# Gates and branch projections by tokens instead of by features in a four-branch mixer, finer attention steps, and another set of durations in the planner's clock

## The chip, the cores and the metric

The kernel runs on one core of a Trainium2 chip. The metric is the device time of one execution in microseconds (us). TensorE (PE) multiplies, with the weight load of each multiplication as a separate instruction (PEld) beside it; VectorE (DVE), ScalarE (ACT) and GpSimd (POOL) do the elementwise work; SyncE (SP) issues the transfers from HBM.

## The reference, cut to what matters

256 tokens with 1024 features go through two layers of one kind (a) and two of another (b). Both kinds have a mixer of four branches, whose outputs are projected to 1024 features, gated, summed and projected again:

```python
# kind a                                        # branches of 512 features
ys = jnp.stack([y_ssm, y_fox, y_moba, y_dsa], axis=2)
proj = jnp.einsum('bsnc,ncd->bsnd', ys, w_branch)
gates = jax.nn.sigmoid(h @ w_gate + b_gate).reshape(bsz, seq, N_BRANCH, D_MODEL)
merged = jnp.sum(gates * proj, axis=2)
return merged @ w_out
...
# kind b                                        # branches of 256 features
o_a = mla_branch(cq, ckv, kpe, positions, mla_norm_q, mla_norm_kv, mla_w_uq, mla_w_ukv)
o_b = spatial_gating_branch(sg_uv, sg_ln_g, sg_ln_b, sg_w, sg_b)
o_c = gla_branch(gq, gk, gv, g_lr, g_og, gla_w_gate, gla_b_gate, gla_norm)
o_d = deltanet_branch(dq, dk, dv, da, db, dz, dn_conv, dn_a_log, dn_dt_bias, dn_norm)
proj = jnp.einsum('bsnw,nwd->bsnd', branches, w_branch)
gate = jax.nn.sigmoid(gates).reshape(b, s, N_BRANCH, D_MODEL)
merged = jnp.sum(gate * proj, axis=2)
return merged @ w_out
```

Kind a then has a SwiGLU layer, kind b a cross attention and a squared-ReLU layer. Three of a's branches and b's `mla_branch` and cross attention are softmax attention over heads of 64.

## The kernel before

**Matrix products.** All of it is fp32. A large product splits each operand in a high and a low part of a reduced fp32 type and takes three passes on PE (high times high, high times low, low times high), so a contraction step of 128 is three matmuls into one PSUM bank. These are the matmuls with `rt` operands in the rows; the small ones of the branches work on `ft` operands in plain fp32. A tile of weights of 128x1024 comes by DMA into one of four `raw` slots, ACT writes its high part (`rt<-raw`), DVE its low part (`rt<-raw,rt`), at most five tiles ahead of PE. A result that becomes the next left operand is split in the same way, by an ACT copy and a DVE subtraction.

**The order of the work** is not written by hand. A planner writes the program twice: it keeps a rough clock (`Model`) that adds up a duration for each instruction (`Engine.cost`, L371, and the transfer's duration in `dma`, L430) and, between the matmuls of large products, takes steps from "lanes", generators that do the branches' small work and `yield` between steps. `spawn` adds such a generator, `drain` runs all of them (or until a flag is set) with no large product between, `flush` runs those of a key. Engines execute in the written order, each its own queue.

**The mixer** (`mix`, L1400) runs for both kinds. It goes through the branches in a fixed order, `ORDER1` = (2, 1, 3, 0) for kind a, `ORDER2` = (1, 0, 2, 3) for kind b, where 2 is GLA and 3 is DeltaNet, and through two halves of 512 output features of each. For a half, `gate` multiplies `h` by the gate weights over 8 contraction steps and `proj` the branch's output over 4 (a) or 2 (b). `proj` begins with `if n not in flags: self.drain(until=lambda: n in flags)`: where the branch isn't ready, its lane is run down first. The products stand with features on partitions: a bank holds two blocks of 128 features by 256 tokens, so a matmul has 256 columns, and a half is two banks (`g2`). The gate's tanh on ACT takes the bias of kind a as a per-partition operand, two instructions of 256 columns for each bank. `stt` on DVE computes (tanh + 1) times the projection out of PSUM. Sums over branches run on POOL, and for the last branch on DVE; `fin` splits the sum into high and low parts as a spawned step with the key `mT0` to `mT3`.

Behind the mixer, `layer_a` and `layer_b` call `self.drain()`, which runs down all lanes; then `out_a` (L1454, token halves of 128, 512 columns) or `out_b` (L2231) multiplies by `w_out`, and flushes the key of each part of the sum before it uses it.

**Attention** (`attention`, L855) takes two heads at a time in a lane step: the second product of pair i-2, the transposes and copies (`pt`) of pair i-1, and the scores, maximum, exponential, reciprocal and scaling of pair i, then one `yield`.

**Head norms** of GLA and DeltaNet (`head_norm`, L1618) go through a matmul, ACT square, DVE reduction, a power on POOL, and DVE scaling, with transposes on PE behind.

Of the kernel before, what the change touches and what calls it, by code (L numbers as in the profile page):

```python
# [9 lines left out]
F32R = mybir.dt.float32r  # L10
# [3 lines left out]
AF = mybir.ActivationFunctionType  # L14
# [3 lines left out]
D = 1024  # L18
# [48 lines left out]
def plan(layer):  # L67
# [9 lines left out]
    if kind == "a":  # L77
# [5 lines left out]
        for i, n in enumerate(ORDER1):  # L83
            for w, c in (("g", 0), ("p", 0), ("g", 1), ("p", 1)):
# [18 lines left out]
    else:  # L103
# [4 lines left out]
        for i, n in enumerate(ORDER2):  # L108
            for w, c in (("g", 0), ("p", 0), ("g", 1), ("p", 1)):
# [242 lines left out]
class Engine:  # L352
# [38 lines left out]
class Kern:  # L391
# [463 lines left out]
    def attention(self, heads, qk, sel, bias, v, dst, done):  # L855
# [16 lines left out]
        for i in range(n + 2):  # L872
# [15 lines left out]
            if 1 <= i <= n:  # L888
# [10 lines left out]
                st[("pt", i - 1)] = pts  # L899
            if i < n:  # L900
# [18 lines left out]
                for j in range(2):  # L919
# [66 lines left out]
    def params(self, layer):  # L986
# [8 lines left out]
        if kind == "a":  # L995
            load("pp", 72, dram["pp1"][l])
# [40 lines left out]
    def layer_a(self, l, hT, pr):  # L1037
# [347 lines left out]
        bg = F.alloc(32, "bg")  # L1385
        self.ts(bg.a, pp[:, 40:72], 0.5, OP.mult)
# [4 lines left out]
        merged = self.mix(L, l, ORDER1, hT, ys, flags, 4, bg.a, load_gains)  # L1391
        bg.free()
# [7 lines left out]
    def mix(self, L, l, order, hT, ys, flags, nkt, bias, load):  # L1400

        F = self.F
        mg, m = {}, []
        halves = [[(256 * g, 256 * g + 128), (256 * g + 128, 256 * g + 256)] for g in range(2)]

        def gate(n, c):
# [19 lines left out]

        def proj(i, n, c, gts):
            if n not in flags:
                self.drain(until=lambda: n in flags)
            for g in range(2):  # L1430
# [1250 lines left out]
```

## Time and profile before

| | |
|---|---|
| median of 3 runs | 2298.11 us (2293.02 to 2301.42) |
| profiled execution | 2296.01 us, span of its trace 2294.2 us |
| mean granted TensorE clock | 0.991 of full speed |
| PE busy | 2237.2 us, 98% |
| PEld busy | 2020.1 us, 88% |
| DVE busy | 1526.5 us, 67% |
| ACT busy | 1074.2 us, 47% |
| POOL busy | 271.2 us, 12% |
| DMA | 375.47 MB, mean 164 GB/s |

PE is busy nearly always, so the time is read as PE's queue: the durations of its instructions, and the places where it stands idle, with what it waited for. All instructions go through one helper, so every row carries L362; what they are is told by engine, operation, tile and shape.

### The profile page before, as it was taken

Reading aid. Unit: us, or ns where it says so; the run is one execution under the profiler, and the core shown is the slowest. Engines: PE = TensorE matmul, PEld = TensorE weight load, DVE = VectorE, ACT = ScalarE, POOL = GpSimd, SP = SyncE. Lnnn points to the kernel's source line nnn. Section 1 sums busy time; section 2 is a strip of 40 time slices with the busy share of each in tenths; the row PEclk is TensorE's granted clock in tenths of the full one; section 3 lists DMA queues with packets and bytes.
Section 4 is the critical chain, followed back from the end, with each engine's and each line's share of the span. In section 5 each row is a group of like instructions: output and inputs, shape, how many; then the busy total and the mean of one; then the engine's idle time right before and its main releaser. Section 6 shows DMA issues by size and latency. Waiting matters only on the chain.

```text
span 2294.2 us, 40097 instructions
## 1 busy us (share of the span) xinstructions
PE 2237.2 (98%) x16244; PEld 2020.1 (88%) x16244; DVE 1526.5 (67%) x2509; ACT 1074.2 (47%) x1695; POOL 271.2 (12%) x244
## 2 busy tenths in 40 slices
PE   7999999999999999999999999999999999999998
PEld 6888998999787899889988899988988889998897
DVE  7786657555888655755588867555557887755554
ACT  4554544444455444544454345444545433544543
POOL 3002120000301112000021321000002132000000
PEclk9999999999999999999999999999999999999999
DMA  6433555555534356565544246456653424644563
GB/s 224 140 122 118 184 183 194 198 182 168 174 118 147 110 166 202 174 228 187 171 132 155 86 131 218 144 177 221 195 165 113 156 94 136 214 155 157 193 204 108
DMA packets 106662, 375.47 MB, mean 164 GB/s; under 512 B 12474, under 2 KB 12908, under 8 KB 106476
## 3 DMA queue, kind: packets, MB, share of 16 engines
q1 hardware_dynamic: 106476, 372.91, 49.4%
q8 instruction: 127, 2.08, 0.4%
q14 instruction: 59, 0.48, 0.1%
HBM read 371.81 MB, written 1.05 MB: 163 GB/s over the span
## 4 chain that ended last, share of the span: by engine, by line
PE 63%; DVE 6%; issue 2%; ACT 1%; DMA 1%; POOL 1%; SPq 0%; POOLq 0%; DVEq 0%; ACTq 0%
PE bank L362 63%; DVE ft L362 4%; DVE rt L362 2%; POOL ft L362 1%; ACT rt L362 1%; ACT ft L362 0%; DMA raw<-in_wts_a 0%; DMA raw<-in_wts_b 0%; DMA ft<-in_positions 0%; POOL qt L362 0%; ACT junk L362 0%; SPq L430 0%; DVE junk L362 0%; POOLq L2676 0%; DVEq L362 0%
## 5 line engine op out<-in xcount | busy, mean ns | idle before, releaser
L362 PE MATMUL bank<-rt 128*128 128x256 f32 (+2 forms) x12720 | 1993.5, 316 | 28.0 <-DVE rt L362 27.7
L362 PEld LDWEIGHTS bank<-rt 128*128 128x128 f32 x12720 | 1781.1, 192 | 186.2 <-DVE rt L362 34.7
L362 DVE TENSOR_TENSOR rt<-raw,rt 128x1024 fp32r<-128x1024 f32 (+2 forms) x692 | 837.5, 1239 | 343.5 <-ACT rt L362 342.3
L362 ACT ACTIVATE rt<-raw 128x1024 fp32r<-128x1024 f32 (+2 forms) x692 | 698.7, 1034 | 410.4 <-PE bank L362 213.5
L362 POOL TENSOR_TENSOR ft<-ft 128x512 f32<-128x512 f32 (+7 forms) x186 | 213.1, 1153 | 1879.7 <-DVE ft L362 1673.5
L362 PE MATMUL bank<-ft 64*64 64x64 f32 (+11 forms) x3476 | 315.6, 266 | 18.8 <-DVE ft L362 12.0
L362 PEld LDWEIGHTS bank<-ft 64*64 64x64 f32 (+6 forms) x3476 | 243.7, 147 | 74.5 <-issue 16.0
L362 ACT ACTIVATE ft<-bank 128x512 f32<-128x512 f32 (+5 forms) x256 | 135.7, 536 | 317.6 <-PE bank L362 290.2
L362 ACT ACTIVATE ft<-ft 128x128 f32<-128x128 f32 (+7 forms) x206 | 87.5, 434 | 182.5 <-DVE ft L362 175.7
L362 DVE SCALAR_TENSOR_TENSOR ft<-ft 128x512 f32<-128x512 f32 (+5 forms) x211 | 93.6, 465 | 42.0 <-ACT junk L362 20.5
L362 DVE TENSOR_TENSOR ft<-ft 128x512 f32<-128x512 f32 (+5 forms) x122 | 68.3, 562 | 63.0 <-ACT ft L362 60.6
L362 DVE SCALAR_TENSOR_TENSOR ft<-bank,ft 128x254 f32<-128x254 f32 (+6 forms) x176 | 80.5, 482 | 24.5 <-PE bank L362 13.9
L362 ACT ACTIVATE rt<-bank 128x512 fp32r<-128x512 f32 (+1 forms) x98 | 53.6, 552 | 85.1 <-PE bank L362 84.1
L362 DVE TENSOR_TENSOR ft<-ft,bank 64x512 f32<-64x512 f32 (+3 forms) x92 | 59.3, 645 | 36.0 <-PE bank L362 29.6
L362 ACT ACTIVATE ft<-bank,ft 128x256 f32<-128x256 f32 x108 | 47.2, 481 | 72.0 <-PE bank L362 48.6
L362 DVE SCALAR_TENSOR_TENSOR ft<-ft,bank 128x512 f32<-128x512 f32 (+1 forms) x106 | 67.6, 642 | 14.6 <-PE bank L362 9.9
L362 DVE COPY ft<-bank 128x384 f32<-128x384 f32 (+6 forms) x96 | 49.4, 542 | 32.9 <-PE bank L362 30.4
L362 DVE TENSOR_SCALAR ft<-ft 128x256 f32<-128x256 f32 (+7 forms) x236 | 55.4, 277 | 21.3 <-ACT ft L362 9.8
L362 ACT ACTIVATE rt<-ft 128x512 fp32r<-128x512 f32 x62 | 39.0, 630 | 65.0 <-DVE ft L362 60.5
L362 DVE TENSOR_TENSOR ft<-bank,ft 128x512 f32<-128x512 f32 (+8 forms) x124 | 50.3, 442 | 16.1 <-PE bank L362 7.5
L362 POOL TENSOR_SCALAR qt<-qt,ft 64x256 fp32r<-64x256 f32 (+1 forms) x32 | 42.1, 1318 | 131.4 <-PE bank L362 130.5
L362 ACT ACTIVATE junk<-ft 128x512 bf16<-128x512 f32 (+1 forms) x46 | 27.2, 591 | 58.1 <-DVE ft L362 55.6
(37 smaller groups left out, 318.6 us busy)
## 6 DMA issues: line engine op xcount, KB each, us to landing
raw<-in_wts_a SPq DMA_DIRECT2D x340, 512.0 KB, 4.4
raw<-in_wts_b SPq DMA_DIRECT2D x312, 512.0 KB, 4.2
raw<-in_wts_b SPq DMA_DIRECT2D x24, 256.0 KB, 2.8
raw<-in_wts_b SPq DMA_DIRECT2D x8, 440.0 KB, 4.2
raw<-in_wts_a SPq DMA_DIRECT2D x8, 340.0 KB, 5.1
ft<-in_mem SPq DMA_DIRECT2D x4, 512.0 KB, 8.3
ft<-in_x SPq DMA_DIRECT2D x2, 512.0 KB, 3.4
ft<-in_norm_mix_pre SPq DMA_DIRECT2D x2, 512.0 KB, 5.3
```

What stands on the lines that cost most here:

```text
L362: r = None if self.dry else f(*args, **kw)
```

## The change

**Shapes.** In the mixer, gates and branch projections stand with tokens on partitions: a bank holds 128 tokens by 512 features, a matmul has 512 columns (`g1` in place of `g2`). Over the program PE has 4224 fewer matmuls of 256 columns and 2112 more of 512. The sum over branches must then be transposed for the next product: `fin` yields once and runs `transpose_to`, in all 16 groups of four 128x128 transposes on PE, each with an ACT copy `rt<-bank` and a DVE subtraction `rt<-bank,rt` (before: the same pair out of SBUF). The keys are by feature half and token half (`mT00` to `mT11`); the output products flush those that a contraction step needs.

**Bias of kind a.** It lies along the columns now: 16 transfers of 512 values, each broadcast to 128 partitions (256 KB in SBUF), issued one gate ahead, and 32 additions of 128x512 on DVE out of PSUM. The tanh is then one ACT instruction of 512 columns for a bank, 32 in all, in place of 64 of 256 columns.

**Order.** Both gates of the last branch come before its two projections (in `plan` and in `mix`).

**Attention.** Two more `yield`s in each lane step: after the `pt` copies, and before the reciprocal.

**The rough clock.** `Engine.cost` gives a 512-column matmul of a large product 226.8 ns in place of 215.3, a 256-column one 120.2 in place of 108.7, and most small plain-fp32 ones less; a transfer takes bytes/400 + 2900 ns in place of bytes/360 + 2000.

```diff
@@ Engine.cost
-            m, n = ins[0].free_size(), ins[1].free_size()
-            one = max(m / 1.2, n / 2.4) + 2
-            return one if ins[0].dtype == F32R else max(112.0, max(2 * m / 1.2, 4 * n / 2.4))
+            rows, m, n = ins[0].shape[0], ins[0].free_size(), ins[1].free_size()
+            if ins[0].dtype == F32R:
+                return max(m / 1.2, n / 2.4 + 12) + 1.5
+            if rows <= 64 and m <= 64:
+                return 68.0
+            share = 0.67 if min(rows, m) <= 64 else 1.0
+            return share * 2 * max(m / 1.2 + 1, n / 1.2 + 2)
@@ dma
-            self.model.op("DMA", out.nbytes() / 360.0, 2000.0, [out], [])
+            self.model.op("DMA", out.nbytes() / 400.0, 2900.0, [out], [])
@@ attention
                 st[("pt", i - 1)] = pts
+                yield
...
                                  accum=nv[:, 1, j, t:t + 1])
+                yield
                 self.V.reciprocal(nm.a[:, 8:12], nm.a[:, 4:8])
@@ mix
-        halves = [[(256 * g, 256 * g + 128), (256 * g + 128, 256 * g + 256)] for g in range(2)]
...
+        steps = [(n, c) for n in order for c in range(2)]
+
+        def fetch(s):
+            if bias is not None and s < len(steps):
+                n, c = steps[s]
+                rows[s] = self.row_at(bias, l, 512, "bg", n * D + c * 512)
...
-            for g in range(2):
+            for t in range(2):
                 b = self.bank()
-                self.g2([b[:, 0:256], b[:, 256:512]], L, f"g{n}{c}", hT, halves[g], 4, g == 1)
+                self.g1(b, L, f"g{n}{c}", hT, t, 4, t == 1)
...
-                    for j in range(2):
-                        ch = n * 8 + c * 4 + g * 2 + j
-                        self.act(gt.a[:, 256 * j:256 * j + 256], b[:, 256 * j:256 * j + 256], AF.Tanh, scale=0.5,
-                                 bias=bias[:, ch:ch + 1])
+                    self.tt(gt.a, b, rows[s].a, OP.add)
+                    self.act(gt.a, gt.a, AF.Tanh, scale=0.5)
...
-        def fin(c, g, s_):
-            yield from self.split(m[c], (slice(None), slice(2 * g, 2 * g + 2), slice(None)), s_.v(2, 256))
+        def fin(c, t, s_):
+            yield "pe"
+            yield from self.transpose_to(s_.a, 4, m[c], t)
             s_.free()
...
-                self.g2([b[:, 0:256], b[:, 256:512]], L, f"p{n}{c}", ys[n][0], halves[g], nkt // 2, g == 1)
-                gt = gts[g]
+                self.g1(b, L, f"p{n}{c}", ys[n][0], t, nkt // 2, t == 1)
+                gt = gts[t]
...
-                    self.spawn(fin(c, g, s_), "mT%d" % (2 * c + g))
...
+                    self.spawn(fin(c, t, s_), "mT%d%d" % (c, t))
+        fetch(0)
+        for s, (n, c) in enumerate(steps[:6]):
+            proj(s // 2, n, c, gate(s))
+            if c:
+                ys[n][0].free()
+        load()
+        gts = [gate(6), gate(7)]
+        hT.free()
+        for c in range(2):
+            m.append(Mat(self, 4, 256, "mT"))
+            proj(3, order[3], c, gts[c])
+        ys[order[3]][0].free()
@@ out_a
-                self.g1(b, L, f"o{c}", m, t, 4, t == 1, wait=lambda p: self.flush("mT%d" % p))
+                self.g1(b, L, f"o{c}", m, t, 4, t == 1, wait=lambda p: self.flush("mT%d%d" % (p // 2, t)))
@@ out_b
-            self.g11(bb, L, f"o{c}", m, 4, lambda p: self.flush("mT%d" % p))
+            self.g11(bb, L, f"o{c}", m, 4, lambda p: [self.flush("mT%d%d" % (p // 2, t)) for t in range(2)])
```

What it moves, at three places. In the rows below, `bank` is a PSUM bank (its number follows), `rt` an operand of a large product, `ft` an fp32 tile.

PE in the first layer b, at the end of the gate ahead of GLA's projection; before:

```order
L362 MATMUL bank_72<-ft 64x256
L362 MATMUL bank_72<-ft 64x64 x4
L362 MATMUL bank_69<-rt 128x256 x6
L362 MATMUL bank_74<-ft 64x128 x2
L362 MATMUL bank_73<-rt 128x256 x18
...
L362 MATMUL bank_73<-rt 128x256 x6
L362 MATMUL bank_68<-ft 128x128 x2
L362 MATMUL bank_73<-rt 128x256 x24
L362 MATMUL bank_75<-ft 128x128 x2
L362 MATMUL bank_70<-rt 128x256 x12
```

And now:

```order
L362 MATMUL bank_75<-rt 128x512 x3
L362 MATMUL bank_74<-ft 128x128 x2
L362 MATMUL bank_72<-ft 128x128 x2
L362 MATMUL bank_69<-ft 128x256
L362 MATMUL bank_73<-ft 128x256
L362 MATMUL bank_70<-ft 128x256
...
L362 MATMUL bank_70<-ft 64x256
L362 MATMUL bank_70<-ft 64x64 x4
L362 MATMUL bank_72<-ft 128x128 x2
L362 MATMUL bank_75<-ft 128x128 x2
L362 MATMUL bank_74<-rt 128x512 x6
```

The small matmuls of GLA and DeltaNet (`ft`) stood between matmuls of the gate; now 26 rows of them, 50 matmuls, stand in one piece between the gate's last three and the projection's first six, and the second layer b has the same piece.

PE at the end of the mixer of the first layer b, from the last projections to `w_out`; before:

```order
L362 MATMUL bank_69<-rt 128x256 x48
L362 MATMUL bank_72<-rt 128x256 x48
L362 MATMUL bank_68<-rt 128x256 x12
L362 MATMUL bank_71<-rt 128x256 x12
L362 MATMUL bank_73<-rt 128x512 x6
```

And now:

```order
L362 MATMUL bank_71<-rt 128x512 x6
L362 MATMUL bank_69<-rt 128x512 x6
L362 MATMUL bank_73<-rt 128x512 x3
L362 MATMUL bank_70<-ft 128x128 x4
L362 MATMUL bank_73<-rt 128x512 x3
L362 MATMUL bank_72<-rt 128x512 x6
L362 MATMUL bank_75<-ft 128x128 x4
L362 MATMUL bank_74<-ft 128x128 x4
L362 MATMUL bank_68<-ft 128x128 x4
L362 MATMUL bank_71<-rt 128x512 x6
```

Ahead of `w_out` (the last row of each) stand four groups of four transposes, three of them behind the last projection. On DVE, the same place now:

```order
L362 SCALAR_TENSOR_TENSOR ft<-ft,bank_71 128x512
L362 TENSOR_TENSOR ft<-ft 128x512
L362 TENSOR_TENSOR rt<-raw,rt 128x1024
L362 SCALAR_TENSOR_TENSOR ft<-ft,bank_69 128x512
L362 TENSOR_TENSOR ft<-ft 128x512
L362 TENSOR_TENSOR rt<-bank_70,rt 128x4x128
L362 SCALAR_TENSOR_TENSOR ft<-ft,bank_73 128x512
L362 TENSOR_TENSOR ft<-ft 128x512
L362 TENSOR_TENSOR rt<-raw,rt 128x1024
L362 SCALAR_TENSOR_TENSOR ft<-ft,bank_72 128x512
L362 TENSOR_TENSOR ft<-ft 128x512
L362 TENSOR_TENSOR rt<-bank_75,rt 128x4x128
```

Each transposed group waits for its gating (`SCALAR_TENSOR_TENSOR`) and addition, and its low part is the `rt<-bank,rt` row.

DVE in an attention of kind a, where the last `ISA` is a maximum of the scores; before:

```order
L362 ISA ft<-bank_69,ft 128x256
L362 ISA ft 128x1
L362 RECIPROCAL ft<-ft 128x4
L362 TENSOR_SCALAR ft<-ft 128x128
L362 TENSOR_SCALAR ft<-ft 128x256
L362 TENSOR_SCALAR ft<-ft 128x128
L362 TENSOR_SCALAR ft<-ft 128x256
L362 TENSOR_TENSOR rt<-raw,rt 128x1024
```

And now:

```order
L362 ISA ft<-bank_71,ft 128x256
L362 ISA ft 128x1
L362 COPY ft<-bank_72 128x384
L362 COPY ft<-bank_68 128x384
L362 TENSOR_TENSOR rt<-raw,rt 128x1024
L362 RECIPROCAL ft<-ft 128x4
L362 TENSOR_SCALAR ft<-ft 128x128
L362 TENSOR_SCALAR ft<-ft 128x256
```

The reciprocal, which needs ACT's exponentials, stood directly behind the maximum at all 28 places of the program, ahead of the next low part of weights (`rt<-raw,rt`); it does so at 1 of 28 now.

## Rows read from the trace of the kernel before

**Rows 1.** The page's engines: busy time, share of the span, instructions.

```profile
PE 2237.2 (98%) x16244; PEld 2020.1 (88%) x16244; DVE 1526.5 (67%) x2509; ACT 1074.2 (47%) x1695; POOL 271.2 (12%) x244
```

**Rows 2.** Waits of PE: total us, count, longest.

```profile
PE bank L362 <- DVE rt L362: 27.7, 20, 3.1
```

**Rows 3.** Stretches of PE's timeline: start, length, what ran, count; [idle before].

```profile
235.45 1.69 PE L362 MATMUL bank<-rt 128*128 128x256 f32 x12
240.25 0.98 PE L362 MATMUL bank<-rt 128*128 128x256 f32 x6 [3.11 <-DVE rt L362]
```

**Rows 4.** DVE's timeline in that idle time.

```profile
237.85 0.18 DVE L362 RECIPROCAL ft<-ft 128x4 f32<-128x4 f32 x1 [1.09 <-ACT ft L362]
238.06 1.01 DVE L362 TENSOR_SCALAR ft<-ft 128x128 f32<-128x128 f32 x4
238.98 1.22 DVE L362 TENSOR_TENSOR rt<-raw,rt 128x1024 fp32r<-128x1024 f32 x1
```

**Rows 5.** Windows: us, busy PE PEld DVE ACT POOL, PEclk, DMA share, GB/s.

```profile
128.80:133.20 4.40, 4.23 (x20) 3.69 (x22) 4.26 (x8) 0.00 (x0) 0.00 (x0) 0.61 0.71 224
...
805.40:812.20 6.80, 6.08 (x28) 5.15 (x29) 2.67 (x5) 2.58 (x9) 0.73 (x1) 0.51 0.23 77
...
1249.70:1251.80 2.10, 0.19 (x3) 0.02 (x1) 2.03 (x5) 1.54 (x2) 0.00 (x0) 1.00 0.00 0
```

**Rows 6.** PE's matmuls by shape: count, busy, mean ns, idle before.

```profile
L362 PE MATMUL bank<-rt 128*128 128x256 f32 x9120 | 1153.9, 286 | 21.3 <-DVE rt L362 21.2
L362 PE MATMUL bank<-rt 128*128 128x512 f32 x3408 | 816.4, 395 | 2.2 <-DVE rt L362 2.1
```

**Rows 7.** PE's timeline, streams without idle time of one shape, and four transposes.

```profile
261.36 0.60 PE L362 MATMUL bank<-ft 128*128 128x128 f32 x4
261.71 68.76 PE L362 MATMUL bank<-rt 128*128 128x256 f32 x571
...
329.83 52.67 PE L362 MATMUL bank<-rt 128*128 128x256 f32 x360
...
2265.37 21.95 PE L362 MATMUL bank<-rt 128*128 128x512 f32 x96
```

**Rows 8.** DVE by shape: count, busy, mean ns, idle before.

```profile
L362 DVE TENSOR_TENSOR rt<-raw,rt 128x1024 fp32r<-128x1024 f32 x652 | 806.3, 1265 | 342.6 <-ACT rt L362 341.4
L362 DVE SCALAR_TENSOR_TENSOR ft<-ft,bank 128x512 f32<-128x512 f32 x90 | 60.9, 682 | 10.8 <-PE bank L362 9.9 <-ACT ft L362 0.7
...
L362 DVE TENSOR_TENSOR ft<-ft 128x512 f32<-128x512 f32 x52 | 36.0, 692 | 50.9 <-ACT ft L362 49.7
...
L362 DVE TENSOR_TENSOR ft<-bank,ft 128x512 f32<-128x512 f32 x38 | 24.7, 684 | 4.1 <-PE bank L362 3.9
...
L362 DVE TENSOR_TENSOR rt<-bank,rt 128x512 fp32r<-128x512 f32 x26 | 17.9, 689 | 29.8 <-ACT rt L362 29.6
```

**Rows 9.** ACT by shape, the same columns.

```profile
L362 ACT ACTIVATE rt<-bank 128x512 fp32r<-128x512 f32 x78 | 46.0, 595 | 66.7 <-PE bank L362 65.9
```

**Rows 10.** The window ahead of GLA's projection in the first layer b, columns of rows 5.

```profile
1340.00:1360.00 20.00, 20.00 (x175) 18.61 (x174) 14.02 (x25) 7.48 (x13) 5.45 (x4) 1.00 0.47 142
```

**Rows 11.** One head norm there: ACT's timeline.

```profile
1353.41 0.38 ACT L362 ACTIVATE ft<-bank 128x256 f32<-128x256 f32 x1 [4.04 <-PE bank L362]
...
1357.63 0.38 ACT L362 ACTIVATE rt<-bank 128x256 fp32r<-128x256 f32 x1 [1.26 <-PE bank L362]
```

**Rows 12.** The same head norm in DVE's timeline.

```profile
1353.83 0.42 DVE L362 TENSOR_REDUCE ft<-ft 128x4 f32<-128x256 f32 x1 [2.06 <-ACT ft L362]
...
1355.64 0.42 DVE L362 TENSOR_TENSOR ft<-bank,ft 128x256 f32<-128x256 f32 x1 [0.25 <-POOL ft L362]
1356.10 0.42 DVE L362 TENSOR_TENSOR ft<-ft 128x256 f32<-128x256 f32 x1
```

**Rows 13.** Its power in POOL's timeline.

```profile
1354.60 1.01 POOL L362 TENSOR_TENSOR ft<-ft 128x4 f32<-128x4 f32 x1 [3.75 <-DVE ft L362]
```

More of the change, by code (lines that the diff above doesn't have):

```diff
@@ L83, in plan @@
         for i, n in enumerate(ORDER1):
-            for w, c in (("g", 0), ("p", 0), ("g", 1), ("p", 1)):
+            for w, c in (("g", 0), ("p", 0), ("g", 1), ("p", 1)) if i < 3 else (("g", 0), ("g", 1), ("p", 0), ("p", 1)):
                 if w == "g":
@@ L108, in plan @@
         for i, n in enumerate(ORDER2):
-            for w, c in (("g", 0), ("p", 0), ("g", 1), ("p", 1)):
+            for w, c in (("g", 0), ("p", 0), ("g", 1), ("p", 1)) if i < 3 else (("g", 0), ("g", 1), ("p", 0), ("p", 1)):
                 if w == "g":
@@ L1390, in load_gains @@
             held["gp"], held["gf"] = self.row_at("norm_mix_post", l, D, "gp"), self.row_at("norm_ffn_pre", l, D, "gf")
-        merged = self.mix(L, l, ORDER1, hT, ys, flags, 4, bg.a, load_gains)
-        bg.free()
+        merged = self.mix(L, l, ORDER1, hT, ys, flags, 4, "b_gate", load_gains)
         self.drain()
@@ L1402, in mix, with gate @@
         F = self.F
-        mg, m = {}, []
-        halves = [[(256 * g, 256 * g + 128), (256 * g + 128, 256 * g + 256)] for g in range(2)]
-        def gate(n, c):
+        mg, m, rows = {}, [], {}
+        steps = [(n, c) for n in order for c in range(2)]
[3 more added lines that the diff above has]
+                rows[s] = self.row_at(bias, l, 512, "bg", n * D + c * 512)
+        def gate(s):
+            n, c = steps[s]
+            fetch(s + 1)
             out = []
-            for g in range(2):
+            for t in range(2):
                 b = self.bank()
-                self.g2([b[:, 0:256], b[:, 256:512]], L, f"g{n}{c}", hT, halves[g], 4, g == 1)
+                self.g1(b, L, f"g{n}{c}", hT, t, 4, t == 1)
                 gt = F.alloc(512, "gt")
@@ L1414, in gate @@
                 else:
-                    for j in range(2):
-                        ch = n * 8 + c * 4 + g * 2 + j
-                        self.act(gt.a[:, 256 * j:256 * j + 256], b[:, 256 * j:256 * j + 256], AF.Tanh, scale=0.5,
-                                 bias=bias[:, ch:ch + 1])
+                    self.tt(gt.a, b, rows[s].a, OP.add)
+                    self.act(gt.a, gt.a, AF.Tanh, scale=0.5)
                 self.fbank(b)
                 out.append(gt)
-            return out
-        def fin(c, g, s_):
-            yield from self.split(m[c], (slice(None), slice(2 * g, 2 * g + 2), slice(None)), s_.v(2, 256))
+            if bias is not None:
+                rows.pop(s).free()
+            return out
+        def fin(c, t, s_):
+            yield "pe"
+            yield from self.transpose_to(s_.a, 4, m[c], t)
             s_.free()
@@ L1429, in proj @@
                 self.drain(until=lambda: n in flags)
-            for g in range(2):
+            for t in range(2):
                 b = self.bank()
-                self.g2([b[:, 0:256], b[:, 256:512]], L, f"p{n}{c}", ys[n][0], halves[g], nkt // 2, g == 1)
-                gt = gts[g]
+                self.g1(b, L, f"p{n}{c}", ys[n][0], t, nkt // 2, t == 1)
+                gt = gts[t]
                 self.stt(gt.a, gt.a, 1.0, b, OP.add, OP.mult)
@@ L1436, in proj @@
                 if i == 0:
[L1437 removed]
+                    mg[(c, t)] = gt
                     continue
[L1439 removed]
+                s_ = mg[(c, t)]
                 self.tt(s_.a, s_.a, gt.a, OP.add, None if i == 3 else self.P)
@@ L1442, in proj @@
                 if i == 3:
-                    self.spawn(fin(c, g, s_), "mT%d" % (2 * c + g))
-        for i, n in enumerate(order):
-            for c in range(2):
-                gts = gate(n, c)
-                if i == 3:
-                    if c == 0:
-                        load()
-                    else:
-                        hT.free()
-                    m.append(Mat(self, 4, 256, "mT"))
-                proj(i, n, c, gts)
-            ys[n][0].free()
+                    self.spawn(fin(c, t, s_), "mT%d%d" % (c, t))
[11 more added lines that the diff above has]
+        ys[order[3]][0].free()
         return Pair(m)
@@ L2637, in arrays @@
         cw = cw.reshape(2, 5, 8, 128).transpose(0, 3, 2, 1).reshape(2, 128, 40)
-        out["pp1"] = np.concatenate([cw, i["b_gate"].reshape(2, 32, 128).transpose(0, 2, 1)], 2)
+        out["pp1"] = cw
+        out["b_gate"] = i["b_gate"]
         out["bc1"] = np.concatenate([i["dt_bias"], i["fox_fbias"], i["a_log"], i["d_skip"], i["ssm_norm"]], 1)
```

6 lines of the change are left out of this document (1 added, 5 removed).

## The prediction

> **What bounds the kernel now.** I read the busy shares first: PE works 2237.2 us of a span of 2294.2, so 57 us are idle; DVE follows with 67% [rows 1]. Then the waits: the largest idle sum of PE is for a low part that DVE writes (`rt`), 27.7 us in 20 waits, none over 3.1 [rows 2]. I went to the longest. At 240.25 PE has run out of weights for 3.11 us [rows 3]. In DVE's queue there stand the reciprocal, which itself waited 1.09 us for ACT's exponentials, then four scalings of 1.01 us in all, and only then the low part that PE wants, 1.22 us [rows 4]. The DVE queue is blocked by a step that waits for ACT, while DVE as a whole has time. Four places have this form (128.85, 240.25, 694.48, 806.12). Last I read the granted clock behind such waits: 0.61 behind the first, 0.51 behind the last [rows 5], so PE ran there mostly at 1.2 GHz instead of 2.4. Everywhere else the time is PE's own queue. A change is worth what it takes from PE's matmuls, or from these few waits, less what new waits it makes.
>
> **Matmul shapes.** Two 256-column matmuls become one of 512, 2112 times. The busy sums of the two shapes, 1153.9/9120 = 126.5 ns and 816.4/3408 = 239.6 ns [rows 6], mix streams with stalls, so I take streams without idle time [rows 7]: 68.76/571 = 120.4 ns for 256 columns, 21.95/96 = 228.6 ns for 512. A pair thus costs 240.8, its successor 228.6: 12.2 ns saved, or 13.4 by the means of rows 6 (2 x 126.5 - 239.6). 2112 x 12.2 = 25.8, x 13.4 = 28.3. I take **-27**.
>
> The rows show 120.4 and 228.6 ns for the issue of back-to-back matmuls in this fp32 stream. The Trainium skill, page "TensorE: Matmul & The Clock Gate", section "Back-to-back issue gap", puts the warm gap near the columns at 2.4 GHz plus 2.5 ns, which as an estimate is 109 and 216 ns: by it a pair would save 2.5 ns, 5 us in all, and the sum below would end some 22 us higher. The rows of this kernel disagree with it at both widths, so the sum goes by them.
>
> **Transposes.** 16 groups of four on PE. One group holds PE from 261.36 to 261.71, 0.35 us [rows 7]: 16 x 0.35 = **+5.6**, on PE's queue wherever they stand.
>
> **The end of the mixer.** Before, PE ran from the last projections into `w_out` without idle time (the 52.67 us of rows 7 from 329.83, which merge 256- and 512-column matmuls). Now the last sum must be gated (`stt` 0.68), added (0.69), transposed, copied by ACT (0.60) and given its low part by DVE (0.69) before `w_out` can start [rows 8, 9], and the drain issues all that before `w_out`'s first matmul. In layers a the last projections are long (12 matmuls a bank, 2.7 us), so that earlier groups are done by then, and DVE's tail is 0.68 + 0.69 + 0.69 less a transposed group, 1.9 us of PE's idle time (bounds 1.0 and 2.5). In layers b a bank is six matmuls, 1.4 us, less than DVE's 1.37 + 0.69 for it: DVE must do four gatings, four additions, two low parts of weights at 1.26 and a low part of 0.69, some 8.7 us, while PE has three further banks and three transposed groups, 3 x 1.36 + 3 x 0.35 = 5.1. That is 3.6 each. 2 x 1.9 + 2 x 3.6 = **+11** (bounds 6 and 16).
>
> **A drain ahead of GLA's projection, in both layers b.** The row order shows 50 small matmuls in one piece with no large product between. Before, they stood between the gate's matmuls, and PE was busy 20.00 of 20.00 us there [rows 10]. What they wait for is now on the path. It is two head norms in sequence, whose length rows show: ACT's square begins at 1353.41 [rows 11], DVE's second scaling ends at 1356.52 [rows 12], 3.1 us with the power on POOL between, 1.01 [rows 13], and behind it come transposes, ACT's copy 0.38 [rows 11] and DVE's low part, as long as a scaling, 0.42: some 4.5 with the hand-overs. 2 x 4.5 = 9. Ahead of the first stand about 15 DVE instructions of GLA's and DeltaNet's states at 0.42 [rows 12], 6.3, and one power waits for another on POOL, some 1.4. In all 16.7, less what PE itself does in it, 50 matmuls at 0.35/4 [rows 7], 4.4: 12.3 idle. The last large matmuls just ahead stand in threes between small ones too; 1.5 more. About 14 for each, **+28** (bounds: 2 x 5, if most of the state work is done when the gate ends, and 2 x 19, if DeltaNet's rows in the same DVE queue wait for PE and ACT in turn). Layers a have no such piece.
>
> **Clock behind the new waits.** After 3 us of waiting the clock was 0.51 to 0.61 for four to seven us [rows 5], so that PE lost about half of these. For four new idle stretches of which two are long: **+5** (0 to 7).
>
> **Attention.** With the new step ends, casts of weights stand between the maximum and the reciprocal at 27 of 28 places. The four waits of 3.1 us then lose their cause, and with them 1 to 3 us each of half clock: 4 x 3.1 + 6, less a part that comes back, since layer a keeps another dense piece of DVE work in its convolution: **-15** (-3, if the next dense piece stalls PE alike, to -19). Near 1250 PE idles 1.91 us in a window in which it is busy 0.19 of 2.10 and DVE 2.03 [rows 5]; that DVE piece is shorter now: **-4** for two layers (0 to -5).
>
> **At nothing.** 32 bias additions at 0.68 [rows 8] are 22 us on DVE, spread over 32 banks of gates, on an engine that works 67% of the time [rows 1]; the tanh behind them has a whole bank's time, 5.5 us, until its projection is gated. 32 tanh of 512 columns in place of 64 of 256 save ACT time, which nobody waits for. The 16 bias transfers are queued on SP one gate, some 11 us, ahead; they add 4 MB to 375. If that cover is gone, a late one holds a gate for 1 to 2 us, and only that gate's tanh. The 16 splits out of PSUM replace equal ones. The rough clock's durations change no work; what they moved is in the rows above.
>
> **Sum**, against the profiled execution of 2296.0 us, 2 us below the median of the runs: 2296 - 27 + 5.6 + 11 + 28 + 5 - 15 - 4 = 2299.6, **2300 us**. Measurements of this kernel tell a difference from none at about 0.5%, 11.5 us, so this is no measurable change.
>
> **Rivals.** *Faster:* the drains cost little. For it: the small work of the branches has been issued all along, so that at the gate's end only one head norm may be left. Then 2 x 5 in place of 28, 6 at the ends of the mixer, 1 of clock and -19 for attention: 2296 - 27 + 5.6 + 10 + 6 + 1 - 19 - 4 = 2269; with the middle of the attention term 2273. It decides for faster when a drain is under 7 us. Against it: both head norms' transposes stand behind the gate's last matmul in PE's queue. *Slower:* the drain is a chain in which DVE, ACT, POOL and PE wait for one another, and two branches share DVE's queue; at 19 us each, 16 at the mixer's ends, 7 of clock and only -6 for attention it is 2296 - 27 + 5.6 + 38 + 16 + 7 - 6 - 2 = 2328. It decides from about 19 us a drain, with most attention waits staying. For it: PE was waiting in no such place before, so nothing there was ever short. *The change does not do what it says:* in the mixer the 512-column stream runs at no less than two of 256 columns, 240 ns, for want of weights; the sum without the 27 is 2327. Against it: the 512-column mean of 239.6 is made of all streams, stalls among them, and 228.6 is measured [rows 6, 7]. The rule of the Trainium skill named above, page "TensorE: Matmul & The Clock Gate", section "Back-to-back issue gap", ends on this side too, at 2321 by its estimate.
>
> **How the numbers follow.** No measurable change, 2287 to 2309: 0.47. Faster, around 2273: 0.25. Slower by long drains, around 2325: 0.25; slower without the saving: 0.03. The likeliest's time is the prediction, 2300. The bounds of all terms together reach from 2266 to 2332; leaving out a tenth at each end I give 2276 to 2321. Faster 0.25, same 0.47, slower 0.28.
>
> **What would show it.** 512-column matmuls of the mixer at 227 to 230 ns without idle time in PE's timeline confirm the first term. One piece of 12 to 17 us in each layer b in which PE does only `ft` matmuls and is idle most of the time confirms the drain; if it is under 7, the sum is too high by up to 20. PE idle for 2 to 4 us right ahead of `w_out`, four times. No wait of PE for `rt` over 2 us in attention; if waits of 3 us remain at its maxima, the attention term is wrong. A granted clock under 0.7 behind a drain shows the clock's term.

## The result and the profile after

The changed kernel takes 2312.03 us (median of 6 runs, 2309.12 to 2318.58) where the kernel before takes 2297.68 us (6 runs): a ratio of 1.007, 95% interval 1.0057 to 1.0083 (the ratios are worked out over all runs and differ a little from those of the medians). It is slower by 14.3 us. The time lies in the range of the prediction and above its 2300, and on the side of "slower by over 0.5%" instead of "no measurable change".

The page of the kernel after, its engines (busy time, share of the span, instructions):

```profile
span 2308.8 us, 36131 instructions
...
PE 2232.7 (97%) x14196; PEld 1911.7 (83%) x14196; DVE 1552.8 (67%) x2539; ACT 1064.4 (46%) x1663; POOL 276.2 (12%) x244
```

PE's busy sum fell by 4.5 us against [rows 1], and its idle time rose from 57.0 to 76.1. The waits of PE after (total us, count, longest):

```profile
PE bank L362 <- DVE ft L362: 37.3, 23, 7.4
...
PE bank L362 <- DVE rt L362: 19.3, 16, 3.8
```

Waits for weights (`rt`) went down from 27.7 [rows 2]; waits for the branches' own data (`ft`) are now the largest sum. They were 12.0 us before:

```profile
PE bank L362 <- DVE ft L362: 12.0, 6, 7.4
```

Which layer gained and which lost is told by the same work reached: PE passes 4,154,496 columns of large products in every version, and the first large product of each layer begins at column 0, 1,081,248, 2,162,496 and 3,158,496. From the starts in PE's timeline, adding up columns, this is how long each layer takes (the last one up to its last large product), and how much less or more than before (us; worked out from one trace of this and of each of the versions below, so that a row can differ by some 2 us from the medians of the runs):

| version | first a | second a | first b | second b |
|---|---|---|---|---|
| before | 580.0 | 581.1 | 556.9 | 558.6 |
| after | -7.1 | -13.6 | +18.2 | +17.5 |
| mixer by tokens alone | -6.3 | -11.2 | +3.1 | +5.8 |
| finer attention alone | -10.0 | -14.8 | +9.3 | +8.0 |
| new durations alone | -1.8 | -4.8 | +17.0 | +13.0 |
| mixer and attention, old durations | -15.9 | -19.2 | +7.0 | +7.0 |

The change wins 21 us in layers a and loses 36 in layers b.

### The profile page after: what moved, and what is told of

Same layout as the page of the kernel before. It is cut to its first block, busy times and chain, and to the rows that moved or that the text cites. A ratio compares the mean times of both kernels' runs of the same rounds, so it can differ in the third digit from the quotient of the medians.

```text
span 2308.8 us, 36131 instructions
## 1 busy us (share of the span) xinstructions
PE 2232.7 (97%) x14196; PEld 1911.7 (83%) x14196; DVE 1552.8 (67%) x2539; ACT 1064.4 (46%) x1663; POOL 276.2 (12%) x244
## 4 chain that ended last, share of the span: by engine, by line
PE 57%; DVE 5%; DMA 2%; issue 2%; POOL 1%; ACT 1%; POOLq 0%; DVEq 0%; ACTq 0%; SPq 0%
PE bank L362 57%; DVE ft L362 3%; DVE rt L362 2%; POOL ft L362 1%; DMA raw<-in_wts_a 1%; DMA raw<-in_wts_b 1%; ACT ft L362 0%; ACT rt L362 0%; DMA ft<-in_positions 0%; ACT junk L362 0%; DVE junk L362 0%; POOLq L2690 0%; DVEq L362 0%; ACTq L362 0%; POOLq L362 0%
## 5 line engine op out<-in xcount | busy, mean ns | idle before, releaser
L362 PE MATMUL bank<-rt 128*128 128x512 f32 (+3 forms) x10608 | 1977.3, 345 | 19.6 <-DVE rt L362 19.3
L362 PEld LDWEIGHTS bank<-rt 128*128 128x128 f32 x10608 | 1657.9, 191 | 253.3 <-DVE rt L362 26.8
L362 PE MATMUL bank<-ft 64*64 64x64 f32 (+13 forms) x3540 | 331.3, 271 | 49.3 <-DVE ft L362 37.3
L362 PEld LDWEIGHTS bank<-ft 64*64 64x64 f32 (+7 forms) x3540 | 257.0, 151 | 133.3 <-DVE ft L362 41.4
L362 ACT ACTIVATE ft<-bank 128x512 f32<-128x512 f32 (+4 forms) x256 | 135.5, 536 | 320.0 <-PE bank L362 303.1
L362 ACT ACTIVATE ft<-ft 128x128 f32<-128x128 f32 (+7 forms) x238 | 107.2, 461 | 257.0 <-DVE ft L362 251.5
L362 DVE TENSOR_TENSOR ft<-bank,ft 128x512 f32<-128x512 f32 (+6 forms) x156 | 72.3, 493 | 38.5 <-PE bank L362 25.4
L362 DVE SCALAR_TENSOR_TENSOR rt<-bank,rt 128x512 fp32r<-128x512 f32 (+1 forms) x72 | 43.4, 613 | 17.6 <-ACT rt L362 17.3
L362 ACT ACTIVATE rt<-ft 128x512 fp32r<-128x512 f32 x46 | 28.9, 629 | 48.1 <-DVE ft L362 46.4
L362 DVE TENSOR_TENSOR rt<-bank,rt 128x512 fp32r<-128x512 f32 x42 | 28.7, 688 | 33.2 <-ACT rt L362 33.1
```

The lines of the kernel that those rows point to most:

```text
L362: r = None if self.dry else f(*args, **kw)
```

## Experiments

### The three parts apart

The change has three parts that can be made alone. Mixer by tokens (shapes, transposes, bias, order of gates), two `yield`s in attention, and the durations. Four versions, run beside the kernel before on one chip. (Beside all the runs of this study the kernel before took 2295.3 to 2297.9 us, so that times of different experiments can be compared to some 2 us.)

```diff
 # clock_only: the kernel before, with
+            if ins[0].dtype == F32R:
+                return max(m / 1.2, n / 2.4 + 12) + 1.5
...
+            self.model.op("DMA", out.nbytes() / 400.0, 2900.0, [out], [])
 # attn_only: the kernel before, with the two yields in attention
 # mix_only: the changed kernel, with the old durations and the old attention
 # mix_attn: the changed kernel, with the old durations
```

> The kernel before with the planner's new durations alone (matmuls and transfers); mixer and attention steps as before. In its order GLA isn't ready ahead of its projection in both layers b: 39 small matmuls stand there in one piece. Theory A (the durations make the late piece, and the piece makes the loss in layers b): slower by 8 to 14 us a layer b, 2310 to 2325, PE idle 5 to 9 us in each piece. Rival B (the loss comes with the mixer by tokens, not with the durations): 2293 to 2303.

Measured: 2321.06 us, beside 2297.81 of the kernel before, ratio 1.0106 (1.0088 to 1.0125). **The durations alone cost 23 us**, though no instruction is added, with 30 lost in layers b and 7 gained in layers a. The time is theory A's, and PE is idle for 6.8 us in the piece of the first layer b, within its 5 to 9. But that is not all that is new there: ahead of the piece PE also waits 3.58 us for weights (at 1248.97), and a loss of 17.0 is more than theory A gave a layer.

> The kernel before with gates and projections by tokens, the transposes and the order of gates, with the old durations and old attention steps. No piece of small matmuls ahead of GLA's projection in its order. Theory A: shapes -27, transposes +6, ends of the mixer +6 to +12, so 2281 to 2290. Rival B: layers b lose some 15 us each as in the changed kernel, layers a gain 5 each: 2310 to 2322.

Measured: 2288.74 us, ratio 0.9965 (0.9952 to 0.9978): 9.1 us faster. Theory A's sum, and rival B falls: layers b lose 3 to 6 each, not 15. By theory A's terms layers b should hardly change, though; why they lose with the mixer alone isn't shown.

> The kernel before with the two further step ends in attention alone. Theory A: the four waits of 3.1 us of PE for a low part of weights go, with the half clock behind them: -15, 2279 to 2287, no wait of PE for weights over 2 us in layers a. Rival B (another dense piece of VectorE stalls PE instead): 2293 to 2300.

Measured: 2287.64 us, ratio 0.9958 (0.9943 to 0.9973): 10.2 us faster, just outside theory A's range and 5 us short of rival B's. By layers it is both theories: layers a gain 24.8, more than was expected, and layers b lose 17.3. One wait for weights of over 2 us is left in layers a, 2.27 us at 977.2. DVE's reciprocals show the gain, here in the kernel after (count, busy, mean ns, idle before):

```profile
L362 DVE RECIPROCAL ft<-ft 128x4 f32<-128x4 f32 x28 | 4.8, 170 | 1.1 <-ACT ft L362 1.1
```

Before, the same row had 30.3 us of idle time before it:

```profile
L362 DVE RECIPROCAL ft<-ft 128x4 f32<-128x4 f32 x28 | 5.0, 178 | 30.3 <-ACT ft L362 30.3
```

DVE no longer stands still for ACT's exponentials. The loss is at the start of a layer b. This is PE's timeline of `attn_only` there (start, length, what, count [idle before]):

```profile
1198.00 0.98 PE L362 MATMUL bank<-rt 128*128 128x256 f32 x6 [1.01 <-DVE rt L362]
1201.45 6.67 PE L362 MATMUL bank<-rt 128*128 128x256 f32 x41 [2.47 <-DVE rt L362]
```

And DVE's queue in that time:

```profile
1195.13 1.75 DVE L362 RECIPROCAL ft<-ft 128x256 f32<-128x256 f32 x1
...
1197.27 0.68 DVE L362 TENSOR_TENSOR rt<-raw,rt 128x512 fp32r<-128x512 f32 x1
1197.87 2.93 DVE L362 SCALAR_TENSOR_TENSOR ft<-bank,ft 128x255 f32<-128x255 f32 x6
1200.72 2.95 DVE L362 TENSOR_TENSOR rt<-raw,rt 128x512 fp32r<-128x512 f32 x3
```

Six steps of DeltaNet's convolution, 2.93 us in one piece, and a reciprocal of 1.75 stand ahead of the low part of weights that PE wants. They are not new. Before, DVE's queue had the same two pieces, the reciprocal at 1220.30 and then

```profile
1222.43 1.89 DVE L362 TENSOR_TENSOR rt<-raw,rt 128x512 fp32r<-128x512 f32 x3
1224.23 2.94 DVE L362 SCALAR_TENSOR_TENSOR ft<-bank,ft 128x255 f32<-128x255 f32 x6
```

and PE waited 0.16 us behind them. Three low parts stood between them then, and one does now, so that PE comes to the end of its weights while the convolution runs. It is a wait of PE for weights behind other work in DVE's queue, as those that went in layers a [rows 3, 4], but DVE does not stand still for ACT in it.

> The changed kernel with the planner's old durations: mixer by tokens and finer attention steps. No piece of small matmuls ahead of GLA's projection in its order. Theory A: the gains of both parts add, 2266 to 2278, 35 to 45 us under the changed kernel. Rival B: as the changed kernel, 2305 to 2315.

Measured: 2274.55 us, ratio 0.9899 (0.9881 to 0.9917): 23.3 us faster than before and 37.5 under the changed kernel. The two gains add (9.1 + 10.2 = 19.3, and 4 more). **All of the slowdown, and more, hangs on the durations.**

### Which durations

```diff
 # new_pe_only: the changed kernel, with
-            self.model.op("DMA", out.nbytes() / 400.0, 2900.0, [out], [])
+            self.model.op("DMA", out.nbytes() / 360.0, 2000.0, [out], [])
 # new_dma_only: the changed kernel, with the old PE part of Engine.cost
```

> The changed kernel with the old duration of transfers in the planner and the new ones of matmuls. Its order has the late piece ahead of GLA's projection in both layers b, 57 small matmuls. Theory A: as the changed kernel or a little worse, 2308 to 2320. Rival C: the matmuls' durations are nearer to the trace than the old ones, so that it is near to the version with old durations, 2272 to 2290.

> The changed kernel with the old durations of matmuls in the planner and the new one of transfers. Its order has a late piece in the second layer b alone (42 small matmuls). Theory A: one piece, so about half way, 2286 to 2298. Rival C: 2272 to 2280, as transfers are hidden.

Measured: 2295.03 us with the matmuls' new durations, ratio 0.9991 (0.9982 to 1.0001), and 2279.61 us with the transfers', ratio 0.9930 (0.9916 to 0.9945). Against 2274.55 that is +20 and +5, where both together cost 37.5. The first run fits neither theory: it has the late piece in both layers b and is 17 us faster than the changed kernel, which has it too. The second is rival C's time and lies under theory A's range, although its second layer b has a piece. So the late piece can't be the whole price of the durations. The same run tells about what one costs: its piece lasts from 1888.09 to 1902.64 with PE idle for 6.8 us, and that layer is 3.3 us longer than in `mix_attn`, while the first layer b, which has no piece, is 0.8 us shorter. That is 3 to 4 us, where a layer b of the changed kernel is 10 to 11 us longer than in `mix_attn`.

### More cover for GLA

```diff
 # cover: the changed kernel, in layers b
-        for s, (n, c) in enumerate(steps[:6]):
+        for s, (n, c) in enumerate(steps[:4]):
             proj(s // 2, n, c, gate(s))
...
+            gts = [gate(4), gate(5)]
+            for c in range(2):
+                proj(2, order[2], c, gts[c])
```

> The changed kernel, but in layers b both gates of GLA come ahead of its two projections, as for the last branch: 24 more matmuls of 512 columns a bank, 11 us, stand between the small steps. In its order the late piece of 50 small matmuls is gone; the durations are still the new ones. Theory A (the late piece costs what layers b lose): 12 to 15 us less a layer b than the changed kernel, 2282 to 2290. Rival C (the new durations cost by many small shifts, the piece only shows them): 2300 to 2312.

Measured: 2311.37 us, ratio 1.0059 (1.0044 to 1.0074), as the changed kernel (2312.03). The expectation was wrong in its premise. The order does still have a piece without large products ahead of GLA's projection, of 28 small matmuls in place of 50, and in the trace PE is idle nearly as long in it. PE's timeline of `cover`:

```profile
1343.56 2.36 PE L362 MATMUL bank<-rt 128*128 128x512 f32 x9
1345.85 1.84 PE L362 MATMUL bank<-ft 128*64 128x128 f32 x24
1350.06 0.68 PE L362 MATMUL bank<-ft 128*128 128x128 f32 x2 [2.37 <-DVE ft L362]
1351.15 3.93 PE L362 MATMUL bank<-ft 128*128 128x128 f32 x22 [0.41 <-DVE ft L362]
1358.28 0.69 PE L362 MATMUL bank<-ft 128*128 128x128 f32 x2 [3.20 <-DVE ft L362]
1358.62 33.28 PE L362 MATMUL bank<-rt 128*128 128x512 f32 x135
```

From 1345.85 to 1358.62 no large product runs: 12.8 us with 6.0 idle, where the changed kernel has 17.3 with 6.8. What is left is the waiting of the last head norms. GLA comes late by more than the cover that this adds. The run doesn't tell the price of a piece that is gone.

### What holds the branches back

The planner takes a branch's step only while the rough clocks of DVE and ACT are at most 2.75 us ahead of PE's (`BACKLOG`). The new durations let PE's clock move less for a small matmul (68 ns for one of at most 64 rows and columns, in place of at least 112; for a large one it moves more), so the limit could bind more often.

```diff
 # after_backlog_4500: the changed kernel; mix_attn_backlog_4500: mix_attn
-BACKLOG = 2750.0
+BACKLOG = 4500.0
 # before_backlog_2000: the kernel before
-BACKLOG = 2750.0
+BACKLOG = 2000.0
```

> The changed kernel with its new durations, and one number of the planner's other: it takes a step of a branch while the rough clocks of VectorE and ScalarE are at most 4.5 us ahead of PE's, in place of 2.75. Theory D (with the new durations PE's rough clock moves less for small matmuls, the other engines look further ahead of it, and this limit holds the branches' steps back until GLA is late): in its order no late piece is left, so 2272 to 2284. Theory E (the new durations cost through shifts in the transfers and casts, and the late piece is a sign): 2300 to 2312, the time lost elsewhere in layers b.

> Mixer by tokens, finer attention, old durations, and this one number at 4.5 us. No late piece in its order with 2.75 either, so if theory D is all that the number does: 2270 to 2278, as with 2.75. If a larger limit lets dense VectorE work stand ahead of casts of weights: 2278 to 2290.

> The kernel before with its old durations and this one number at 2.0 us in place of 2.75. In its order a piece of 30 small matmuls without a large one stands ahead of GLA's projection in both layers b. Theory D: slower by 6 to 14 us a layer b, 2310 to 2326. Theory E: within 5 us of the kernel before.

Measured: 2299.96 us for the changed kernel with 4.5, ratio 1.0016 (1.0008 to 1.0025), 12 us faster than with 2.75 and above theory D's range. 2289.56 us for the old durations with 4.5, ratio 0.9963 (0.9952 to 0.9975), 15 us *slower* than with 2.75. And 2322.91 us for the kernel before with 2.0, ratio 1.0115 (1.0101 to 1.0130), 27 us slower, with 33 lost in layers b and 5 gained in layers a.

The last one shows that the kernel before can be made to lose as layers b of the changed kernel do, with this limit alone. It doesn't show that the piece of 30 small matmuls is how: in the first layer b of its trace PE waits 7.4 us for weights and 3.6 for the branches' data, where the kernel before has 2.4 and none. The first two show that the limit trades two things. PE's timeline of `after_backlog_4500`, first at the start of the first layer b, then ahead of GLA's projection:

```profile
1209.04 1.22 PE L362 MATMUL bank<-rt 128*128 128x512 f32 x2 [4.01 <-DVE rt L362]
...
1243.38 2.50 PE L362 MATMUL bank<-rt 128*128 128x512 f32 x5 [5.68 <-DVE rt L362]
...
1340.47 2.20 PE L362 MATMUL bank<-ft 128*128 128x128 f32 x22
1345.96 0.41 PE L362 MATMUL bank<-ft 128*128 128x128 f32 x2 [3.29 <-DVE ft L362]
```

The piece is down to 24 records of matmuls (the changed kernel has 90) and 5.6 us, but two waits of 4.01 and 5.68 us for weights are there, longer than any in the kernels before and after. More of the branches' DVE work is let in ahead of the casts. By layers this version stands at -10.3, -15.0, +18.4 and +13.3 against before: with the piece cut to a third the first layer b loses as much as with 2.75 (+18.2), and of the 8.6 us that the two traces differ by, 4.6 come in layers a. That is against theory D, which had the 12 us and more in layers b; the time lies at the edge of theory E's. The old durations with 4.5 came out in the range given for dense DVE work ahead of casts, and their trace has a wait of 4.67 us for weights in the first layer b.

With 4.5 in both, the new durations cost 10.4 us (2299.96 - 2289.56), with 2.75 in both 37.5. So limit and durations belong together, but 15 of the 27 us between these two are what the limit of 4.5 costs the old durations, and 12 what it gives the new ones.

### The end of the mixer

```diff
 # mix_attn_tail: mix_attn, behind the mixer of both kinds
-        self.drain()
+        self.drain([n for n in self.lanes if not str(self.keys.get(n)).startswith("mT")])
```

> The kernel with mixer by tokens, finer attention and old durations, and the drains behind the mixer leave the transposes of the sum to the flushes of the output product, so that in layers b its first steps stand between the last transposes. Expected if the ends of the mixer are drains' waits (1.2 and 1.9 us idle a layer b, half clock behind them, and 1 to 2 us a layer a): 2262 to 2270. If the output product waits for the first transposes alike: 2271 to 2276.

Measured: 2272.36 us, ratio 0.9896 (0.9880 to 0.9912), beside 2274.55: in the range for an output product that waits for the transposes alike, and a difference of 2 us that the runs don't tell from none. In PE's timeline of `mix_attn` the end of the mixer in the first layer b is

```profile
1370.49 0.63 PE L362 MATMUL bank<-ft 128*128 128x128 f32 x4 [1.20 <-DVE ft L362]
1373.02 0.63 PE L362 MATMUL bank<-ft 128*128 128x128 f32 x4 [1.90 <-DVE ft L362]
```

and in `mix_attn_tail`

```profile
1370.08 0.66 PE L362 MATMUL bank<-ft 128*128 128x128 f32 x4 [1.81 <-DVE ft L362]
1372.03 4.21 PE L362 MATMUL bank<-rt 128*128 128x512 f32 x9 [1.29 <-DVE rt L362]
```

3.1 us idle in both. In layers b the output product's first step needs the first two transposed groups and their low parts, and those end last; the drain was not what PE waited for. The gating, adding and casting on DVE is. In layers a it was the drain. The wait of 1.67 us ahead of the last transposes, which `mix_attn` has in both,

```profile
347.00 0.66 PE L362 MATMUL bank<-ft 128*128 128x128 f32 x4 [1.67 <-DVE ft L362]
```

is gone in both with the drain, since matmuls of the output product stand between the groups:

```profile
346.44 2.62 PE L362 MATMUL bank<-rt 128*128 128x512 f32 x9
348.90 0.60 PE L362 MATMUL bank<-ft 128*128 128x128 f32 x4
```

The gain of 2 us is about what these two waits would be worth, but the runs don't tell it from none.

### Layers a alone

```diff
 # a_layers_only: mixer by tokens and finer attention in layers a, old durations;
 # in layers b the mixer of before, and in attention
+                if self.fine:
                     yield
```

> Mixer by tokens and finer attention steps in layers a alone, old durations; layers b as in the kernel before, whose order on TensorE it has there nearly row for row. Theory F (what layers a gain and layers b lose stand apart, by the same work reached: layers a 16.5 and 18.9 us earlier with both parts and old durations, layers b 7 us later each): 2259 to 2266. Theory G (the lead that layers a gain is given back in layers b, since the transfers and casts come no sooner there): 2270 to 2282.

Measured: 2262.66 us beside 2295.32, ratio 0.9852 (0.9835 to 0.9868): **32.7 us faster than the kernel before and some 49 faster than the changed one**, the best of all versions. By layers: -14.7, -17.8, +2.0, -0.1. Theory F. What layers a gain stays, and what mixer and attention cost layers b comes from what they do in layers b. (The new durations were not tried in one kind of layer alone.) PE's waits in it sum to 16.4 us for weights and 14.7 for the branches' data, both under those of the kernel after (19.3 and 37.3).

## Why the prediction was right in its range and wrong in its middle

**Matmul shapes, right.** A long stream in the first layer a after, and a transposed group:

```profile
265.74 79.95 PE L362 MATMUL bank<-rt 128*128 128x512 f32 x352
345.53 0.60 PE L362 MATMUL bank<-ft 128*128 128x128 f32 x4
345.88 2.32 PE L362 MATMUL bank<-rt 128*128 128x512 f32 x9
```

79.95/352 = 227.1 ns a matmul where 228.6 was taken, and two of 256 took 240.8 [rows 7]: 13.7 ns a pair, 2112 times, 28.9 us for 27. The busy sums of the two shapes, which have the stretches at half clock in them, fell by less, 20.7 us, from 1970.3 [rows 6] to 1949.6:

```profile
L362 PE MATMUL bank<-rt 128*128 128x512 f32 x5520 | 1333.9, 396 | 4.3 <-DVE rt L362 4.0
L362 PE MATMUL bank<-rt 128*128 128x256 f32 x4896 | 615.7, 286 | 10.2 <-DVE rt L362 10.2
```

The rule of the Trainium skill that was weighed there ("TensorE: Matmul & The Clock Gate", "Back-to-back issue gap"), which that section gives for a matmul by itself and not for a stream of weight loads and matmuls, would have made it 5. The trace after disagrees with it, as that before did.

**Transposes and the ends of the mixer, right in size.** 345.88 - 345.53 = 0.35 us a group, as taken. The ends were put at 1.9 us idle in a layer a and 3.6 in a layer b:

```profile
351.44 0.66 PE L362 MATMUL bank<-ft 128*128 128x128 f32 x4 [1.67 <-DVE ft L362]
...
1396.40 0.63 PE L362 MATMUL bank<-ft 128*128 128x128 f32 x4 [1.20 <-DVE ft L362]
1398.93 0.69 PE L362 MATMUL bank<-ft 128*128 128x128 f32 x4 [1.90 <-DVE ft L362]
```

1.67 and 3.10. (The prediction's own terms, 0.68 + 0.69 + 0.69 - 0.35, make 1.71 and not 1.9.) The cause named for the idle time, the drain, holds in layers a and not in layers b (`mix_attn_tail`).

With the shapes the mixer's part was forecast at -27 + 5.6 + 11 = -10.4, and `mix_only` measured -9.1. That the sum is so near is in part luck. Of the 2112 pairs 576 are in each layer a and 480 in each layer b, so the terms give -4 for a layer a and -1 for a layer b; measured were -6.3 and -11.2, +3.1 and +5.8. And PE's busy sum in `mix_only` is 13.0 us under that of before (2224.2 for 2237.2), where -27 + 5.6 was taken, while its idle time is up by 3.9 us (60.9 for 57.0), where 11 was taken.

**The drain ahead of GLA, there, and sized too long in idle time.** PE's timeline after, the first layer b:

```profile
1333.17 0.38 PE L362 MATMUL bank<-ft 128*128 128x128 f32 x2
1335.19 3.08 PE L362 MATMUL bank<-ft 128*128 128x128 f32 x30 [1.63 <-DVE ft L362]
1339.79 0.71 PE L362 MATMUL bank<-ft 64*128 64x128 f32 x4 [1.52 <-DVE ft L362]
1341.40 5.72 PE L362 MATMUL bank<-ft 128*64 128x128 f32 x50 [0.90 <-DVE ft L362]
1349.11 0.44 PE L362 MATMUL bank<-ft 128*128 128x128 f32 x2 [1.99 <-DVE ft L362]
1350.32 0.44 PE L362 MATMUL bank<-ft 128*128 128x128 f32 x2 [0.78 <-DVE ft L362]
1350.52 41.74 PE L362 MATMUL bank<-rt 128*128 128x512 f32 x183
```

The piece lasts 17.3 us (16.7 were forecast for its chain), and in the second layer b 18.5. Of that PE is idle 6.8 us, not 12.3 and not most of the time: the records have 90 matmuls where the order counts 50, and PE is at half clock in part. The windows (columns as in [rows 5]):

```profile
1333.20:1350.50 17.30, 10.48 (x91) 7.93 (x90) 10.56 (x30) 4.16 (x9) 4.94 (x5) 0.90 0.00 1
```

I took 28 for both layers and 5 for the clock. The durations cost the layers b 11.2 and 10.5 (after less `mix_attn` in the table of layers: 18.2 - 7.0 and 17.5 - 7.0), 21.7 in all. The piece is only a part of that: where one stood alone (`new_dma_only`), it cost 3 to 4 us, not 14. What I had at nothing is that the durations cost **layers a** 8.8 and 5.6 us: in their order no piece of small matmuls stands out, and so I gave them no term. One place of it is the norm between the two layers a. PE after:

```profile
580.34 1.97 PE L362 MATMUL bank<-ft 128*128 128x128 f32 x8 [4.14 <-DVE ft L362]
```

In `mix_attn` the same transposes wait 0.57 us:

```profile
571.68 1.32 PE L362 MATMUL bank<-ft 128*128 128x128 f32 x8 [0.57 <-DVE ft L362]
```

In DVE's queue after, two additions that wait for PE now stand ahead of the norm's last small step (`128x1`), which POOL and then the transposes wait for:

```profile
576.30 1.29 DVE L362 TENSOR_TENSOR ft<-bank,ft 128x512 f32<-128x512 f32 x2 [1.25 <-PE bank L362]
577.51 0.15 DVE L362 SCALAR_TENSOR_TENSOR ft<-ft 128x1 f32<-128x1 f32 x1
```

In `mix_attn` that step stands ahead of the additions:

```profile
570.05 0.16 DVE L362 SCALAR_TENSOR_TENSOR ft<-ft 128x1 f32<-128x1 f32 x1
...
572.21 1.28 DVE L362 TENSOR_TENSOR ft<-bank,ft 128x512 f32<-128x512 f32 x2
```

Another is the start of the first layer a, where PE waits 3.83 us for weights at 20.40 (1.45 before). Together the durations cost 37.5 where 28 + 5 stood in the sum. This nearness is luck: the terms were for layers b, which lost 21.7, and the 14.4 of layers a made up for what was missing. By kind, against `mix_attn` with the same 14196 matmuls, PE's idle time is 22.3 us longer (76.1 for 53.8) and its busy time 13.7 (2232.7 for 2219.0), at a granted clock of 0.985 for 0.992. The clock's term, 5, was too small.

**Attention, the step that failed.** The sum had -15 for layers a and -4 for the heads of layers b, "that DVE piece is shorter now". Layers a gained more, 24.8 in `attn_only`. Layers b lost 17.3 where 4 of gain were written. I read the places where PE waited before, found their cause gone, and didn't ask what DVE would do instead in layers b, where PE had few waits to lose. (The longest wait for weights before was not the one at 240.25 but another of 3.14 us at 1002.60, in which DVE waits for ACT's high part; it was not of the form that went.) With finer attention steps, the convolution's six steps stand in front of casts that PE wants next. In the kernel after, that wait is 2.62 us, and the window behind it runs at 0.82 (columns as in [rows 5]):

```profile
1197.00:1207.50 10.50, 7.90 (x63) 7.43 (x61) 8.17 (x20) 6.32 (x17) 0.00 (x0) 1.00 0.29 98
1207.50:1217.00 9.50, 9.46 (x47) 8.19 (x47) 8.59 (x24) 4.78 (x11) 2.41 (x2) 0.82 0.55 178
```

Forecast -19, measured -10.2: nine of the twelve us between 2300 and 2312 are this term. The others are the durations' 37.5 for 33 (+4.5), the mixer's -9.1 for -10.4 (+1.3), the median of before 1.7 above the profiled execution, and 4 us that mixer and attention gain together beyond their sum.

**The range.** It held the result, but it was drawn narrower than the chances beside it: 2276 to 2321 leaves out the middle of both rivals, 2273 and 2325, which had 0.25 each.

**The rivals.** The slower one, long drains with little gain from attention, came nearest in sign and in half of its mechanism: the attention gain was small, not because its waits stayed but because others came. Its drains of over 19 us of idle time did not come. The bias transfers, their additions and the longer tanh cost nothing that a wait of PE shows.

**What stays open.** How the price of the new durations splits in layers b, and why the matmuls' and the transfers' new durations, 20 and 5 us alone, make 37.5 together. The traces show two places. The wait of 4 us at the norm between the layers a stands in all four versions with both new durations, and in none of the two with one of them. And in the kernel after and in `cover` PE waits 3.3 us for POOL in each layer b, here in the first (the longest such wait in layers b of another version is 2.52 us, in `mix_attn_backlog_4500`):

```profile
1269.46 3.16 PE L362 MATMUL bank<-ft 64*64 64x64 f32 x32 [3.33 <-POOL ft L362]
```

Some 10 us at about half clock follow it (the last section), so that by estimate it costs some 8 us a layer b; with 3 to 4 for the late piece that would be near the 11.2 and 10.5. No run takes this wait away alone. `new_pe_only`, which has the piece and not this wait, still loses 7.4 and 6.2 us in layers b against `mix_attn`, so the account isn't shown.

## What to carry to other kernels

When a planner orders the work, its constants are a change of their own, to be timed alone: durations nearer to the trace made the program 37.5 us slower (a matmul of 512 columns had 215.3 ns, then 226.8 where 227.1 was measured; a transfer of 512 KB had 3.5 us, then 4.2 where the page of the kernel before has medians of 4.2 and 4.4 from issue to landing). A limit beside them moves with them: at 4.5 us it gave the new durations 12 us and cost the old ones 15. Cut a step finer where the trace shows the engine that bounds the kernel wait for it, and only there. DVE stood behind ACT's exponentials in layers b too (1.03 and 1.37 us at 1199.94 and 1208.89, before), but PE waited for that in layers a alone: the same cut gained 25 us there and lost 17 in layers b. Compare versions by the same work reached, layer by layer; a sum of -21 and +36 hides what a version with -33 needs.

## What the runs showed of the hardware

The half clock lasted longer behind a wait than the rows of before had shown. In the kernel after PE waited 3.33 us for POOL, and then 10.5 us of small matmuls (64x64) and some large ones ran at a granted clock of 0.51, thus at 1.2 GHz for nearly all of it, with PE busy throughout:

```profile
1264.00:1269.50 5.50, 2.17 (x26) 1.50 (x22) 3.21 (x7) 0.53 (x2) 2.76 (x3) 1.00 0.51 157
1269.50:1280.00 10.50, 10.50 (x105) 8.34 (x106) 3.70 (x8) 2.14 (x3) 2.56 (x2) 0.51 0.05 21
```

In the second layer b the same wait, 3.37 us, was followed by 10.5 us at 0.57. Before, waits of 3.0 and 3.1 us were followed by 4.4 and 6.8 us at 0.61 and 0.51 [rows 5]. I had taken one to three us of loss for a wait; here it is about five by estimate (half of 10.5).
